# A gated convolution-and-pooling trunk in float32r: the input projection of paired blocks by seven partial products

## The chip, the cores and the metric

The kernel runs on one core of one Trainium2 chip. The metric is device time in microseconds (us) of one execution. Of the core's engines five matter here: TensorE (PE; its weight loads are listed apart as PEld), VectorE (DVE), ScalarE (ACT), GpSimd (POOL) and SyncE (SP). Transfers are issued by SP, ACT or POOL and carried by 16 DMA engines.

## The reference, cut to what matters

There are 1104 tokens: 16 meta tokens and 1024 prompt tokens in one sequence, and 8 samples of 8 tokens. The model width is 1024. One layer is computed:

```
h = RMSNorm(x)                                  # per token, over 1024 channels
z = h @ w_in                                    # 1024 -> 7168, split into seven groups of 1024:
#   a_val | a_gate | a_silu | p_in | p_silu | g_a | g_b
u = a_val * sigmoid(a_gate)                     # GLU
c = causal depthwise conv of u, width 31        # state of 30 positions in front
A = (silu(LayerNorm(c)) * silu(a_silu)) @ w_conv_out
pooled = trailing mean of p_in over 2/4/8/16 positions, minus p_in
B = ((pooled @ w_pool_mix per group) * pool_scale * silu(p_silu)) @ w_pool_out
y = RMSNorm(x + (sigmoid(g_a) * A + sigmoid(g_b) * B) @ w_out)
```

The last 30 values of u and the last 15 of p_in go out as new states. Everything is float32.

## The kernel before

Channels lie on the 128 partitions and tokens along the columns, except in the output projection. Every product is made of three float32r products: a float32 operand is split into a high part (rounded to float32r) and a low part (the remainder), and high x high, high x low and low x high are summed in PSUM. `split` (L97) does that with a ScalarE copy and a VectorE subtraction.

w_in is cut into 56 blocks of 128 output channels, 8 for each of the seven groups. `gemm` (L123) makes one block: 8 chunks of 128 input channels x 3 products x 3 pieces of the tokens, 72 matmuls of 368 columns (all tokens: GLU and pool input) or 364, 362 and 362 columns (without the meta tokens: gates). A block's weights come by one transfer of 512 KB into a tile with two buffers; their two parts have three buffers each. The products of one block fill a PSUM tile of three banks, of which there are two.

In order of the program: the first five pool-input blocks (`NX`) multiply x times the norm's gain, and take the token's factor 1/rms after the product, because the sum over the squares is not ready yet; the statistic is made by small matmuls at `STATS_AT`, and spread over the partitions by others at `SPREAD_AT` (`root_stats` L155, `spread` L169). Then x is normalised and split once for all other blocks (L271 to L276). Then come the pooling branch (`pool_in`, `pool_gates`, `pool_mix`), and blocks in the order that `ORDER` (L42) writes out: GLU with convolution (`glu` L390, `conv_chunk` L367, 30 multiply-adds of 1024 columns and 30 of 64 for each of 8 chunks on VectorE), branch B times its merge gate (`branch_b`), merge gate of A, SiLU path. Results for later wait in DRAM (`d_tb`, `d_sga`). LayerNorm, the merge projection and the output projection with tokens on partitions (`project` L545, matmuls of 512 columns) follow.

The instructions of one engine run in the order in which they were queued. Inside `manual_schedule` that is the program's order; elsewhere a scheduler places what is ready by priority (program order), and `later()` lowers the priority of the convolution by 4000, so that it fills the gaps of VectorE. Tiles of 4.4 KB per partition ("slots", 38) come from one pool.

Of the kernel before, what the change touches and what calls it, by code (L numbers as in the profile page):

```python
# [7 lines left out]
F32 = mybir.dt.float32  # L8
F32R = mybir.dt.float32r
AF = mybir.ActivationFunctionType  # L10
ALU = mybir.AluOpType

P = 128
D = 1024
NK = D // P
META = 16
# [7 lines left out]
TP2 = SEQ  # L24
# [3 lines left out]
# Columns of a PSUM tile's three banks: of all tokens, and of all but the meta tokens. Counts are even.  # L28
CUT1 = (0, N1, 2 * N1, TALL)
CUT2 = (0, 364, 726, T2)  # L30
EW = CB + TP + DB * (CB + DS)
PW = TP + DB * (PB + DS)
# [3 lines left out]
NSLOT = 38  # L36
CONV_LATER = 4000
WARM = 8
NX = 5
STATS_AT, SPREAD_AT = (2, 5), (2, 7)  # L40
# c: GLU and convolution, b: branch B, a: merge gate of A, s: SiLU path of A.
ORDER = "c0 b0 c1 b1 b2 c2 b3 b4 c3 b5 b6 c4 b7 a0 c5 a1 a2 c6 a3 a4 c7 a5 a6 a7 s0 s1 s2"  # L42
# [7 lines left out]
def hybrid_trunk_kernel(  # L50
# [25 lines left out]
    wp = ctx.enter_context(tc.tile_pool(name="wp", bufs=3))  # L76
# [3 lines left out]
    ps3 = ctx.enter_context(tc.tile_pool(name="ps3", bufs=2, space=bass.MemoryType.PSUM))  # L80
    ps1 = ctx.enter_context(tc.tile_pool(name="ps1", bufs=2, space=bass.MemoryType.PSUM))

    def slot(name, n=T2, dt=F32):
        return sl.tile([P, n], dt, tag="slot", name=name, bufs=NSLOT, padded_shape=[P, TALL])

    def bank3(name):
        return ps3.tile([P, 3, 512], F32, tag="bank3", name=name)

    pv = const.tile([P, NPAR], F32, name="pv")
    ident = const.tile([P, P], F32, name="ident")  # L90
    ones = const.tile([P, P], F32, name="ones")
    pool.memset(ones, 1.0 / D)
# [8 lines left out]
    def load_w(src, name):  # L101
        raw = wp.tile([P, NK, P], F32, tag="raw", name=f"raw_{name}", bufs=2)
        h = wp.tile([P, NK, P], F32R, tag="wh", name=f"wh_{name}")
        l = wp.tile([P, NK, P], F32R, tag="wl", name=f"wl_{name}")
        sp.dma_start(out=raw, in_=src)

        def ready():
            split(h, l, raw)
            return h, l

        return ready

    def load_w_now(src, name):
        return load_w(src, name)()
# [7 lines left out]

    def gemm(out, w, xs, c0, cut, ns=range(3), nk=NK, m0=0, ks=None):  # L123
        wh, wl = w
        xh, xl = xs
        for k in ks or range(nk):
            for i, (a, b) in enumerate(((wh, xh), (wh, xl), (wl, xh))):
                for j in ns:
                    pe.matmul(  # L129
                        out[:, j, : cut[j + 1] - cut[j]],  # L130
                        a[:, k, m0 : m0 + P],
                        b[k][:, c0 + cut[j] : c0 + cut[j + 1]],
                        start=(k == 0 and i == 0),
                        stop=(k == nk - 1 and i == 2),
                    )
# [5 lines left out]
    def pieces(ps, t):  # L141
        n, m = CUT2[1], CUT2[2] - CUT2[1]
        return (ps[:, 0, :n], t[:, :n]), (ps[:, 1:, :m], v3(t[:, n:], m))
# [6 lines left out]
    def token_tiles(n):  # L150
        return [min(i * P, n - P) for i in range((n + P - 1) // P)]
# [3 lines left out]
    def root_stats(ssum, n, eps, name):  # L155
        tiles = token_tiles(n)
        nt = len(tiles)
        ps = ps1.tile([P, 512], F32, tag="ps1", name=f"pst_{name}")
        for i, lo in enumerate(tiles):
            pe.matmul(ps[:, 2 * i : 2 * i + 2], ssum[:, lo : lo + P], ones[:, :2], start=True, stop=True)  # L160
        a, r, t = (sm.tile([P, 2 * nt], F32, tag=f"ir{x}", name=f"ir{x}_{name}", bufs=1) for x in "art")
        dve.tensor_scalar(a, ps[:, : 2 * nt], eps, None, ALU.add)
        act.activation(r, a, AF.Sqrt)
        dve.reciprocal(r, r)
        refine(r, a, t)
        return r

    # The factors of root_stats with tokens along the columns, on every partition.
    def spread(r, n, name):  # L169
        tiles = token_tiles(n)  # L170
        nt = len(tiles)
        out = slot(f"ir_{name}", n)
        for g in range(0, nt, 4):
            ps = ps1.tile([P, 512], F32, tag="ps1", name=f"pb_{name}{g}")
            part = tiles[g : g + 4]
            dg = slot(f"dg_{name}{g}", 4 * P)
            for i, lo in enumerate(part):
                d = dg[:, i * P : (i + 1) * P]
                dve.tensor_scalar(d, ident, r[:, 2 * (g + i) : 2 * (g + i) + 1], D, ALU.mult, ALU.mult)
                pe.matmul(ps[:, i * P : (i + 1) * P], ones, d, start=True, stop=True)  # L180
            if len(part) == 4:
                act.copy(out[:, part[0] : part[0] + 512], ps)
            else:
                for i, lo in enumerate(part):
# [481 lines left out]
```

## Time and profile before

| | |
|---|---|
| time, median of 3 runs | 1014.71 us (1014.0 to 1014.74) |
| span of the profiled execution, first to last instruction | 1011.5 us |
| PE busy | 1000.9 us, 5838 matmuls |
| DVE busy | 716.7 us |
| ACT busy | 261.1 us |
| POOL busy | 13.4 us, 29 instructions |
| moved by DMA | 79.02 MB, mean 78 GB/s |

The profiled execution is known by its span; the runs are timed around it, and their median is 3.2 us longer than that span. Busy time is the union of the instructions of an engine; a matmul's own duration (some 330 ns) overlaps the next one's, so the pace of a stream of matmuls is read from the chain, as a stretch's duration over its count.

### The profile page before, as it was taken

Reading aid. Unit: us, or ns where it says so; the run is one execution under the profiler, and the core shown is the slowest. Engines: PE = TensorE matmul, PEld = TensorE weight load, DVE = VectorE, ACT = ScalarE, POOL = GpSimd, SP = SyncE. Lnnn points to the kernel's source line nnn. Section 1 sums busy time; section 2 is a strip of 40 time slices with the busy share of each in tenths; the row PEclk is TensorE's granted clock in tenths of the full one; section 3 lists DMA queues with packets and bytes.
Section 4 is the critical chain, followed back from the end, with each engine's and each line's share of the span. In section 5 each row is a group of like instructions: output and inputs, shape, how many; then the busy total and the mean of one; then the engine's idle time right before and its main releaser. Section 6 shows DMA issues by size and latency. Waiting matters only on the chain.

```text
span 1011.5 us, 13769 instructions
## 1 busy us (share of the span) xinstructions
PE 1000.9 (99%) x5838; PEld 978.2 (97%) x5838; DVE 716.7 (71%) x918; ACT 261.1 (26%) x344; POOL 13.4 (1%) x29
## 2 busy tenths in 40 slices
PE   8999999999999999999999999999999999999997
PEld 7999999999999999999999999999999999997885
DVE  6697753544999959769689799999846934445343
ACT  7644232222211111111121111111245722114111
POOL 0001100000000000000000000000000000000000
PEclk9999999999999999999999999999999999999999
DMA  8222222231212222221221232322111033334322
GB/s 276 68 38 63 61 49 49 45 68 39 48 65 52 90 51 83 69 48 64 70 48 64 68 93 49 101 45 90 64 42 43 23 149 131 130 131 174 124 77 84
DMA packets 45374, 79.02 MB, mean 78 GB/s; under 512 B 22912, under 2 KB 28032, under 8 KB 45312
## 3 DMA queue, kind: packets, MB, share of 16 engines
q1 hardware_dynamic: 43008, 69.22, 23.8%
q10 hardware_dynamic: 2304, 8.91, 2.6%
q8 instruction: 46, 0.75, 0.3%
q14 instruction: 16, 0.13, 0.0%
HBM read 63.09 MB, written 15.03 MB: 77 GB/s over the span
## 4 chain that ended last, share of the span: by engine, by line
PE 96%; DMA 1%; DVE 1%; SPq 0%; issue 0%; ACT 0%; DVEq 0%
PE pg L129 10%; PE pv L129 10%; PE psl L129 9%; PE ppo L129 9%; PE pps L129 9%; PE pga L129 9%; PE pgb L129 9%; PE pco L129 9%; PE pp L129 9%; PE pwo L549 7%; PE pmix L129 2%; DMA raw_wo<-in_w_out 1%; PE pwos L549 1%; DMA raw_p<-in_w_in 1%; DVE wol L99 0%
## 5 line engine op out<-in xcount | busy, mean ns | idle before, releaser
L378 DVE SCALAR_TENSOR_TENSOR c<-ce,pv,c 128x1024 f32<-128x1024 f32 x240 | 307.6, 1283 | 3.1
L379 DVE SCALAR_TENSOR_TENSOR c<-ce,pv,c 128x64 f32<-128x64 f32 x240 | 68.0, 283 | 5.6 <-ACT c L376 1.5
L500 DVE TENSOR_TENSOR lga<-pco,lga 128x364 f32<-128x364 f32 (+1 forms) x16 | 10.8, 719 | 46.8 <-PE pco L129 46.8
L129 PE MATMUL pg<-hh,wh_g 128*128 128x368 f32 x192 | 42.7, 330 | 0.0
L129 PE MATMUL pv<-hh,wh_v 128*128 128x368 f32 x192 | 42.6, 330 | 0.0
L129 PE MATMUL psl<-hh,wl_s 128*128 128x362 f32 (+1 forms) x192 | 42.6, 329 | 0.0
L129 PE MATMUL pg<-hl,wh_g 128*128 128x368 f32 x192 | 42.6, 330 | 0.0
L129 PE MATMUL psl<-hh,wh_s 128*128 128x362 f32 (+1 forms) x192 | 42.6, 329 | 0.0
L129 PE MATMUL pg<-hh,wl_g 128*128 128x368 f32 x192 | 42.6, 330 | 0.0
L129 PE MATMUL pv<-hh,wl_v 128*128 128x368 f32 x192 | 42.5, 330 | 0.0
L129 PE MATMUL pv<-hl,wh_v 128*128 128x368 f32 x192 | 42.5, 329 | 0.0
L129 PE MATMUL ppo<-ql,wh_po 128*128 128x362 f32 (+1 forms) x192 | 42.4, 329 | 0.0
L129 PE MATMUL pps<-hh,wl_ps 128*128 128x362 f32 (+1 forms) x192 | 42.4, 329 | 0.0
L129 PE MATMUL pga<-hh,wl_ga 128*128 128x362 f32 (+1 forms) x192 | 42.4, 329 | 0.0
L129 PE MATMUL pgb<-hh,wl_gb 128*128 128x362 f32 (+1 forms) x192 | 42.3, 328 | 0.0
L129 PE MATMUL ppo<-qh,wl_po 128*128 128x362 f32 (+1 forms) x192 | 42.3, 329 | 0.0
L129 PE MATMUL pco<-cxh,wh_co 128*128 128x362 f32 (+1 forms) x192 | 42.3, 328 | 0.0
L129 PE MATMUL pps<-hl,wh_ps 128*128 128x362 f32 (+1 forms) x192 | 42.2, 328 | 0.0
L129 PE MATMUL pgb<-hl,wh_gb 128*128 128x362 f32 (+1 forms) x192 | 42.2, 328 | 0.0
L129 PE MATMUL pga<-hl,wh_ga 128*128 128x362 f32 (+1 forms) x192 | 42.2, 328 | 0.0
L129 PE MATMUL psl<-hl,wh_s 128*128 128x362 f32 (+1 forms) x192 | 42.2, 328 | 0.0
L129 PE MATMUL pco<-cxl,wh_co 128*128 128x362 f32 (+1 forms) x192 | 42.2, 328 | 0.0
(212 smaller groups left out, 2210.9 us busy)
## 6 DMA issues: line engine op xcount, KB each, us to landing
x<-in_xT SPq DMA_DIRECT2D x24, 184.0 KB, 4.0
d_tb<-gbo ACTq DMA_DIRECT2D x8, 544.0 KB, 2.8
d_sga<-gao ACTq DMA_DIRECT2D x8, 544.0 KB, 3.4
t<-d_tb SPq DMA_DIRECT2D x8, 544.0 KB, 4.5
lga<-d_sga SPq DMA_DIRECT2D x8, 544.0 KB, 5.6
raw_ps<-in_w_in SPq DMA_DIRECT2D x8, 512.0 KB, 3.5
raw_g<-in_w_in SPq DMA_DIRECT2D x8, 512.0 KB, 4.2
raw_v<-in_w_in SPq DMA_DIRECT2D x8, 512.0 KB, 3.5
```

The costliest lines, as they stand in the source:

```text
L129: pe.matmul(out[:, j, : cut[j + 1] - cut[j]], a[:, k, m0 : m0 + P], b[k][:, c0 + cut[j] : c0 + cut[j + 1]], start=(k == 0 and i == 0), sto ...
L378: dve.scalar_tensor_tensor(cp, sp_, wk, cp, ALU.mult, ALU.add)
L379: dve.scalar_tensor_tensor(cs, ss_, wk, cs, ALU.mult, ALU.add)
L500: dve.tensor_tensor(c, p, c, ALU.mult)
L549: pe.matmul(ps[:, n - ns[0], :], x(k), w[k][:, n * 512 : (n + 1) * 512], start=(k == 0 and s == 0), stop=(k == NK - 1 and s == len(passes) ...
```

## The change

Blocks are taken in pairs. Two output blocks, two halves of the input channels (4 chunks each) and two halves of the tokens make a 2 x 2 x 2 product; it is computed by seven products of half size in place of eight (Winograd's form of Strassen's scheme). Columns of tokens are reordered into two halves of 552 (8 meta, 512 prompt and 32 sample tokens each), and a matmul takes half of one half: 276 columns, 272 without the meta tokens.

- Seven token operands ("11", "T3", "21", "T2", "T1", "22", "T4"), with 4 chunks each, are made once after RMSNorm, as sums and differences of the four quarters, and split into two parts: 28 tiles, each of which fills one of now 35 slots.
- Seven weight operands are made for each pair (`w_ops`): two sums by a transfer that adds to its destination, two by VectorE.
- `split_dma` takes the low part by an accumulating transfer from the GpSimd queue: ScalarE writes the high part, then its negative, and the transfer adds the source.
- The products are completed by three PSUM tiles x, y, v of two banks. y starts as ScalarE's copy of x. Two quarters end in PSUM (y after "21", x after "22"), the other two are v combined by VectorE with copies of x taken on the way (c2, c4).
- Six pool-input blocks (four together for the first token half) run plain ahead of the norm's factor; 25 pairs follow, interleaved by hand on PE so that the next pair's first product stands inside the current pair.
- The statistic is now a product with a matrix of ones over full width and its inverse root by logarithm and exponential on ScalarE (`totals`, `inv_root`).
- All of the input projection comes first; pool inputs, gates, SiLU paths and convolution outputs go through DRAM. Mixing, branch B, LayerNorm, merge and output projection follow, on half token ranges (272 columns); their operands are split by `split_dma` as well, except those of the output projection.
- The sample's convolution is a product with a window of 31 and a reduction; the convolution's sum over channels chunks is an accumulating transfer into DRAM.

The core of the diff:

```diff
+    def split_dma(dst_h, dst_l, src):
+        act.copy(dst_h, src)
+        act.mul(dst_l, dst_h.bitcast(F32), -1.0)
+        pool.dma_start(out=dst_l, in_=src, accum_op=ALU.add)
...
-NSLOT = 38
-CONV_LATER = 4000
+NSLOT, NWS, NOP, NZ = 35, 11, 6, 8
+CONV_LATER = 6000
-NX = 5
+NX = 6
+ORDER = "g0 p3 q0 q1 q2 g1 q3 b0 b1 g2 b2 b3 a0 g3 a1 a2 a3 s0 s1 s2 s3"
...
+UNITS1 = ((0, HT // 2), (HT // 2, HT))
+UNITS2 = ((HM, HM + H2 // 2), (HM + H2 // 2, HT))
+UNITS3 = ((0, H2 // 2), (H2 // 2, H2))
...
+    for k in range(NQ):
+        xa, xb = xs[k], xs[NQ + k]
+        dve.scalar_tensor_tensor(xa, xa, col(OFF_NG, k), rms, ALU.mult, ALU.mult)
+        t_split("11", k, xa[:, 0])
+        dve.scalar_tensor_tensor(xb, xb, col(OFF_NG, NQ + k), rms, ALU.mult, ALU.mult)
+        s3, s1, s2, s4 = (half(f"ts{i}{k}") for i in (3, 1, 2, 4))
+        dve.tensor_tensor(s3, xb[:, 1], xa[:, 1], ALU.subtract)
+        t_split("T3", k, s3)
+        dve.tensor_tensor(s1, xa[:, 0], xa[:, 1], ALU.subtract)
+        dve.scalar_tensor_tensor(s2, s1, -1.0, xb[:, 1], ALU.mult, ALU.subtract)
+        t_split("T2", k, s2)
+        t_split("21", k, xb[:, 0])
+        t_split("T1", k, s1)
+        dve.scalar_tensor_tensor(s4, s2, -1.0, xb[:, 0], ALU.mult, ALU.subtract)
+        t_split("22", k, xb[:, 1])
+        t_split("T4", k, s4)
...
+    def w_ops(src, name):
+        a, b, q3, q1, d, q2, q4 = (half_raw(f"{x}_{name}") for x in ("a", "b", "q3", "q1", "d", "q2", "q4"))
+        (a_, b_), (c_, d_) = ((x[:, :NQ], x[:, NQ:]) for x in src)
...
+        sp.dma_start(out=a, in_=a_)
+        sp.dma_start(out=q3, in_=a_)
+        pool.dma_start(out=q3, in_=c_, accum_op=ALU.add)
+        sp.dma_start(out=q1, in_=c_)
+        pool.dma_start(out=q1, in_=d_, accum_op=ALU.add)
+        sp.dma_start(out=b, in_=b_)
+        sp.dma_start(out=d, in_=d_)
+        yield op("a", a)
+        yield op("q3", q3)
+        dve.tensor_tensor(q2, q1, a, ALU.add)
+        yield op("q2", q2)
+        yield op("b", b)
+        yield op("q1", q1)
+        dve.tensor_tensor(q4, q2, b, ALU.add)
+        yield op("q4", q4)
+        yield op("d", d)
...
+        x = bank2(f"px_{name}")
+        product_of(x, "11", True, False)
+        yield
+        y = bank2(f"py_{name}")
+        act.copy(y[:, :, :n], x[:, :, :n])
+        v = bank2(f"pv_{name}")
+        yield
+        product_of(v, "T3", True, False)
+        product_of(x, "T2", False, False)
+        c2 = keep("c2")
+        product_of(y, "21", False, True)
+        put(0, 0, y[:, :, :n])
+        product_of(x, "T1", False, False)
+        c4 = keep("c4")
+        yield
+        dve.scalar_tensor_tensor(c4, v[:, :, :n], -1.0, c4, ALU.mult, ALU.subtract)
+        product_of(x, "22", False, True)
+        put(0, 1, x[:, :, :n])
+        yield
+        put(1, 1, c4)
+        product_of(v, "T4", False, True)
+        dve.scalar_tensor_tensor(c2, v[:, :, :n], -1.0, c2, ALU.mult, ALU.subtract)
+        put(1, 0, c2)
...
+    with tc.manual_schedule(engines={pe.engine}):
+        cur = pairs[0]
+        next(cur), next(cur)
+        for nxt in pairs[1:] + [None]:
+            next(cur)
+            if nxt:
+                next(nxt)
+            next(cur)
+            if nxt:
+                next(nxt)
+            next(cur, None)
+            cur = nxt
...
+        for h in range(2):
+            ps = bank2(f"{name}{h}")
+            gemm(ps, w, lambda k, s: xs[k][h][:, s], UNITS3, tuple(range(nk)), True, True)
+            use(h, ps[:, :, : H2 // 2])
```

In each `product_of`, 4 chunks x 3 products x 2 pieces are 24 matmuls. A letter of `ORDER` is now a pair of blocks: g two sets of seven products (gate and value of the GLU), p, q, b, a, s one. `half_raw` has 11 buffers (`NWS`), the split weight operands 6 (`NOP`).

## Rows read from the trace of the kernel before

**Rows 1.** page, part 1: busy us, share of the span and instructions of each engine
```profile
PE 1000.9 (99%) x5838; PEld 978.2 (97%) x5838; DVE 716.7 (71%) x918; ACT 261.1 (26%) x344; POOL 13.4 (1%) x29
```

**Rows 2.** chain of waits in order of time: start, duration, what (x matmuls)
```profile
40.88 1.90 PE pst_x L160 x18
...
45.93 2.05 PE pb_x L180 x18
...
289.98 12.07 PE pv L129 x72
302.05 11.96 PE pgb L129 x72
...
811.69 95.38 PE pco L129 x576
...
952.08 7.43 PE pwos L549 x32
```

**Rows 3.** busy time by stretch; its column line is shown first
```profile
core 0: us, PE busy (x) PEld busy (x) DVE busy (x) ACT busy (x) POOL busy (x), PEclk, DMA share, GB/s
0.00:5.00 5.00, 3.78 (x16) 3.49 (x16) 0.29 (x1) 2.20 (x4) 0.41 (x5) 1.00 0.49 131
5.00:8.00 3.00, 2.74 (x11) 1.94 (x12) 2.22 (x6) 1.67 (x5) 0.00 (x0) 1.00 0.85 248
8.00:13.00 5.00, 3.40 (x17) 2.29 (x15) 2.77 (x7) 3.38 (x7) 0.00 (x0) 1.00 0.93 311
13.00:25.00 12.00, 12.00 (x71) 11.86 (x72) 11.03 (x21) 11.14 (x21) 0.00 (x0) 1.00 0.95 335
...
230.00:746.00 516.00, 516.00 (x3096) 516.00 (x3095) 434.29 (x573) 87.66 (x106) 4.67 (x12) 1.00 0.23 64
...
1004.00:1011.50 7.50, 0.08 (x1) 0.00 (x0) 2.89 (x9) 0.93 (x3) 0.00 (x0) 0.78 0.19 71
```

**Rows 4.** instruction groups of ScalarE by form: busy, mean ns | idle before
```profile
L98 ACT CAST hh<-x 128x1104 fp32r<-128x1104 f32 x8 | 8.4, 1115 | 0.0
...
L334 ACT ACTIVATE gate<-pps 128x364 f32<-128x364 f32 x8 | 3.7, 467 | 0.0
...
L163 ACT ACT_TABLE_LOAD x2 | 2.6, 1283 | 0.0
L98 ACT CAST mh<-mraw 128x512 fp32r<-128x512 f32 x4 | 2.5, 621 | 4.7 <-DMA mraw<-in_w_mix 4.6
```

**Rows 5.** instruction groups of VectorE by form
```profile
L378 DVE SCALAR_TENSOR_TENSOR c<-ce,pv,c 128x1024 f32<-128x1024 f32 x240 | 307.6, 1283 | 3.1
L379 DVE SCALAR_TENSOR_TENSOR c<-ce,pv,c 128x64 f32<-128x64 f32 x240 | 68.0, 283 | 5.6 <-ACT c L376 1.5
...
L272 DVE SCALAR_TENSOR_TENSOR x<-x,pv,ir_x 128x1104 f32<-128x1104 f32 x8 | 10.3, 1365 | 2.6 <-ACT ir_x L185 2.6
...
L542 DVE TENSOR_SCALAR xr<-xr,s 128x1024 f32<-128x1024 f32 x7 | 5.3, 753 | 0.2
...
L99 DVE TENSOR_TENSOR ml<-mraw,mh 128x512 fp32r<-128x512 f32 x4 | 2.7, 684 | 0.0
```

**Rows 6.** GpSimd in order of time: start, duration, instruction, count
```profile
25.82 0.52 POOL L289 COPY pe<-pst 128x120 f32<-128x120 f32 x2 [24.88 <-DMA pst<-in_spool]
...
109.94 1.49 POOL L289 COPY pe<-pst 128x120 f32<-128x120 f32 x1 [22.92 <-DMA raw_ps<-in_w_in]
...
302.03 0.39 POOL L404 COPY ce<-cst 128x240 f32<-128x240 f32 x1
...
632.63 2.39 POOL L404 COPY ce<-cst 128x240 f32<-128x240 f32 x1
```

**Rows 7.** DMA issues by line: count, KB of each, median us from issue to landing
```profile
mraw<-in_w_mix SPq DMA_DIRECT2D x4, 256.0 KB, 4.3
...
out<-xr SPq DMA_DIRECT2D x2, 256.0 KB, 2.2
```

More of the change, by code (lines that the diff above doesn't have):

```diff
@@ L15 @@
 NK = D // P
+NQ = NK // 2
 META = 16
@@ L148, in refine @@
         dve.scalar_tensor_tensor(r, t, 1.5, r, ALU.add, ALU.mult)
[L150 to L165, printed above, removed]
-        return r
@@ L169, in spread @@
[L169 to L182, printed above, removed]
-            else:
-                for i, lo in enumerate(part):
-                    act.copy(out[:, lo : lo + P], ps[:, i * P : (i + 1) * P])
-        return out
@@ new lines, in hybrid_trunk_kernel, with keep_raw, plain @@
+    for i in range(NF, NX):
+        for lo in (0, NQ):
+            load_first(i, lo, lo + NQ)
+    for k in range(NK):
+        load_x(k, 1, full)
+    def keep_raw(j, h, ps):
+        z = half(f"rawp{j}{h}")
+        act.copy(v3(z, HT // 2), ps[:, :, : HT // 2])
+        sp.dma_start(out=d_raw[j][:, h], in_=z)
+    def plain(out, w, h, ks):
+        gemm(
+            out,
+            lambda k, s: w[s][:, k],
+            lambda k, s: xg[h][k][:, s],
+            UNITS1,
+            ks,
+            ks[0] == 0,
+            ks[-1] == NK - 1,
+        )
@@ new lines, in product, with seven, product_of, keep @@
+    def product(out, w, t, units, first, last):
+        gemm(out, lambda k, s: w[:, s, k], lambda k, s: t[k][:, s], units, tuple(range(NQ)), first, last)
+    def seven(src, name, units, put):
+        ws = w_ops(src, name)
+        n = units[0][1] - units[0][0]
+        def product_of(out, t, first, last):
+            product(out, next(ws), t_ops[t], units, first, last)
+        def keep(what):
+            z = half2(f"{what}_{name}", 2 * n)
+            act.copy(z, x[:, :, :n])
+            return z
+        x = bank2(f"px_{name}")
[21 more added lines that the diff above has]
+        put(1, 0, c2)
@@ L326, in pool_gates @@
[L326 to L339 removed]
+            s2 = slot(f"pw{j}_{d}", (TP,))
@@ new lines, in flat, with pool_pair, put @@
+    def flat(z):
+        return z.rearrange("p a b -> p (a b)")
+    def pool_pair(i):
+        ext = [pool_ext(2 * i + b) for b in range(2)]
+        done = [0, 0]
+        def put(b, h, z):
+            j = 2 * i + b
+            if not b:
+                t = half2(f"zp{j}{h}", HT)
+                act.copy(t, z)
+                z = t
+            r, o = parts(flat(z)), ext[b][2](h)
+            act.copy(o[1], r[1])
+            pool.tensor_copy(o[0], r[0])
+            act.copy(o[2], v3(r[2], DS))
+            done[b] += 1
+            if done[b] == 2:
+                with later():
+                    pool_window(j, *ext[b][:2])
+        return [seven((w_in[PG + 2 * i], w_in[PG + 2 * i + 1]), f"p{i}", UNITS1, put)]
@@ L340, in pool_mix @@
+    q = []
+    for g in range(4):
+        pooled = [halves(fetch(d_pool[j], f"lp{j}"), f"pool{j}") for j in (2 * g, 2 * g + 1)]
+        mraw = slot(f"mraw{g}", (2, 2 * P))
         sp.dma_start(out=mraw, in_=w_mix[g])
-        wm = [wp.tile([P, 2, 2 * P], F32R, tag=f"m{x}", name=f"m{x}{g}", bufs=1) for x in "hl"]
-        split(wm[0], wm[1], mraw)
-        for i, gate in enumerate(gates):
+        wm = op_tile(f"m{g}", (2, 2, 2 * P))
+        split(wm[:, 0], wm[:, 1], mraw)
+        for i in range(2):
```

699 lines of the change are left out of this document (370 added, 329 removed).

## The prediction

> **What bounds the kernel now.** I read the busy shares first: TensorE is at work for 1000.9 of 1011.5 us, VectorE for 716.7, ScalarE for 261.1, GpSimd for 13.4 [rows 1]. A busy share does not say at what pace, so the chain of waits in order of time came next. It runs through matmuls from end to end, and gives paces: a block of 72 matmuls takes 12.07 us with 368 columns (168 ns each) and 11.96 us with 364, 362 and 362 (166.1 ns), 32 matmuls of 512 columns take 7.43 us (232.2 ns) [rows 2]. Busy time by stretch shows where PE is not fed: it starts at 5.0 us, lacks 1.9 us until 13 us, and is done 7.4 us before the end; its granted clock is 1.00, the level of 2.4 GHz, in every stretch but the last [rows 3]. So the end is set by the number of matmuls times their pace, and only these can give time. Summed: 24 blocks x 12.09 + 32 x 11.96 = 672.9 us input projection; branch B and merge projection 191.4; mixing 23.9; output projection 416 x 0.2322 = 96.6; statistics 9.7; together 994.5. With 5.0 of start, 7.4 of tail and 4.6 of gaps that is the span, 1011.5. The median of the runs is 3.2 us longer than the span; I add that at the end.
>
> **The pace of shorter matmuls.** This is the first disputed term, because the change cuts 1104 columns into four pieces in place of three: 6528 matmuls of 272 or 276 columns, and no row has that width. At 2.4 GHz 276 columns need 115.0 ns. The three paces lie 15.0, 14.7 and 18.9 ns above their columns' time [rows 2]. A line through 362.7 and 512 columns gives 5.6 + 0.4426 per column: 127.7 ns at 276, 126.0 at 272. In proportion to the 166.1 ns it would be 126.4 and 124.6; with a fixed 15 ns on top, 130.0 and 128.3. A floor set by loading the weights lies lower: 18 matmuls with 128 x 128 weights and 2 columns took 1.90 us, 105.6 ns each, and 18 of 128 columns (float32) 2.05 us, 113.9 ns [rows 2]. I take the line.
>
> **TensorE's new sum.** Six plain blocks: 6 x 96 = 576 x 127.7 = 73.6 us. A set of seven products has 7 x 24 = 168 matmuls; 9 sets for all tokens (8 GLU, 1 pool) 1512 x 127.7 = 193.1; 16 sets for gates 2688 x 126.0 = 338.7. So the input projection falls from 672.9 to 605.4, though the matmul count for it goes from 4032 to 4776. Branch B and merge 1536 x 126.0 = 193.5, mixing 24.2, output projection 96.6 as before, three column sums 3.0. Total 922.7, 71.8 less than before. By proportional paces 913.7, with the fixed 15 ns 938.
>
> **Start.** Four blocks begin together on 4.5 MB of weights and half of x. The rate reached 335 GB/s at a 0.95 share of the engines [rows 3]; PE's 24.5 us on these blocks need 184. The first chunk comes as before; the second waits for 1.7 MB. I keep 5.0 and 4.6 us, and 1 more.
>
> **The joint where the token operands are made.** PE's own work from 5 us: four blocks of the first half until 33, two more until 45, two blocks of the second half until 57, column sums, then four half blocks until 82.5. The square sums are ready before 57 (ScalarE 8 x 1.12 us after scaling and copies). After the sums' matmuls at 58 come two copies, Ln, Exp and Square of 1104 columns (1.115 us each, by [rows 4], and up to two table loads of 1.283), and four VectorE operations of 0.8 to 1.4 us [rows 5]: the norm's factor is there at about 70. Then each of 4 chunks needs seven operands, each with two ScalarE operations of 552 columns. From 621 ns at 512 columns and 1115 at 1104 [rows 4] one takes 0.654 us, an operand 1.31. The order is by chunk, so the first product ("11", four chunks) waits for the 22nd operand: 71.4 + 22 x 1.31 = 100.2, and for its transfer, 2.2 to 4.3 us for 256 KB [rows 7], so 103. VectorE needs only 5.4 us per chunk and is not the limit. PE runs dry at 82.5: 20 us of stall. Lower bound 5 (the scheduler takes "11" first, and operands follow at PE's pace, 3.1 us per product), upper 45 (weight splits and copies of raw blocks go between, 6 us, and transfers take twice as long). I take 20.
>
> **The sets in steady state.** A set lasts 21.2 to 21.5 us on PE. ScalarE: 14 split operations of 512 columns x 0.621 = 8.7, one copy PSUM to PSUM, two out of PSUM, four activations at 0.62 to 0.65 (467 ns at 364 columns and the slope above [rows 4]) = 4.5; 13.2 us, 62%. VectorE: two weight sums and two combinations, some 2.8 us; the convolution as before 308 us, the sample's taps some 43 in place of 68 [rows 5], windows 54, GLU products 11; together 487 of the 532 us of all sets. The last two chunks (88 us) come in reach with 7 sets (148 us) to go, so LayerNorm is not late. A product takes 3.1 us, and that is the cover of each copy that PE waits for: c2 is taken while "21" runs, c4 and the next y while the next pair's "11" or "T4" runs. Behind a split that waits for its weights these copies queue on ScalarE; before, such waits cost PE nothing from 230 to 746 us [rows 3], with covers four times as long. I take 10 us for all 25 sets, bounds 0 and 50.
>
> **The accumulating transfers, the second disputed term.** No row has one. A gate set moves plainly five weight loads of 262 KB and four results of 278 KB, 2.42 MB, and adds nine times 262 KB, 2.36 MB. At 335/0.95 = 353 GB/s [rows 3] that is 6.9 us plus 6.7 us times f, f being the price of an added byte against a copied one. An add has one stream more to read: f of 1 to 2 is what I expect, and up to 20.3 us of 21.2. I cost it at nothing on the path, with f open up to 3 for the range.
> GpSimd issues nine of these per set, 324 in all, where it had 29 instructions. Its copies of 120 columns took 0.26 us when VectorE was between jobs and 1.49 in the pooling windows; one of 240 took 0.39 or 2.39 beside the convolution [rows 6]. Nine times 0.26 to 2.39 is 2.3 to 21.5 us, within a set. Behind a waiting issue stand the other operands' issues, but six split operands are five products ahead.
> The Trainium skill (SBUF — State Buffer, "Who interferes with whom") says that a VectorE instruction with two SBUF inputs holds up a GpSimd instruction that reads SBUF, while descriptor writing is held up only by VectorE's two-port modes. The stretched copies agree with its first half; that the issues stay short beside the convolution no row here shows. By that rule issuing would be near the 2.3 us, and the sum is unchanged.
>
> **Mixing, merge, end.** Splits of pooled inputs and of q take 16 x 4 x 0.65 = 42 us of ScalarE around 24 us of PE; a third can be done ahead, since the 28 operand tiles leave seven slots until the last products free more. I take 8 us of stall (0 to 20). Branch B's 97 us cover LayerNorm and A's splits (65 us of ScalarE). Output weights come late for the same lack of slots: 2 us (0 to 10). Tail 7.4.
>
> **Sum.** 922.7 + 5.0 + 5.6 + 20 + 10 + 8 + 2 + 7.4 = 980.7 of span, and 3.2: 984. Its own range, from the bounds of the stalls and paces taken singly, is 950 to 1010.
>
> **Rivals.**
> *Everything hides* (0.14): proportional pace 913.7, a stall of 5 at the operands, 3 elsewhere: 942. For it speaks that PE lost nothing at any joint before [rows 3]; against it ScalarE's 28.8 us at the operands.
> *The transfers become the bound* (0.11): PE waits in each set. It is slower than before once f passes 2.3: gate sets then take 22.3 us (16 x 1.1 = 18) and the operands, 22 x 283 KB, 41 in place of 29 us (+12), which is the whole gain of 31. At f = 3 it is 16 x 5.8 + 9 x 2.4 + 24 = 138 more, 1122. For it: nine of eighteen transfers of a set are of a kind without a row; against it: the share was 0.23 in the steady part [rows 3].
> *Issuing on GpSimd binds* (0.06): at 2.39 us each [rows 6] the sets just keep pace, but the operands' 22 issues take 53 us and not 29: with 5 at the sets, 1013, no change.
> *The pace does not fall* (0.04): each nanosecond per short matmul is 6.5 us, so at 132.4 ns for 276 columns the gain is gone; at 145 it is 1097. The row at 105.6 ns speaks against it.
> *The joints add up* (0.07): operands 45, sets 40, mixing 20 us: 1051.
>
> **How the numbers follow.** The forecast holds 0.58. Faster by over 0.2%, which is about what a measurement tells from no change: 0.58 + 0.14 and a third of the GpSimd case, 0.74; within 0.2%: 0.03; slower 0.23. The range of 8 in 10 reaches from 945 to 1060: it leaves out the transfers' case beyond f = 2.6, half of the unchanged pace and a third of the lowest case, 0.18.
>
> **What would show it.** Pace: 168 matmuls of a gate set in 21.2 us, in the chain. Operands: an idle stretch of PE near 20 us before the first "11", ended by ScalarE or a transfer. Sets: PE idle per set under 0.5 us, DMA share under 0.9. Wrong: PE idle in every set and ended by a transfer (f too high) or by ScalarE (its queue), or 132 ns and more per matmul.

## The result: slower, 1671 us, and the profile after

The changed kernel takes 1671.28 us (median of four executions, 1657.32 to 1677.56); the kernel before, beside it, 1014.63. The ratio is 1.6451 [1.638, 1.6522]. The profiled execution took 1672.76 us, with a span of 1671.0.

Busy time of each engine from the page of the kernel after, the line that answers to [rows 1]:

```profile
PE 1019.5 (61%) x6960; PEld 980.7 (59%) x6960; DVE 663.3 (40%) x807; ACT 560.5 (34%) x934; POOL 299.1 (18%) x370
```

TensorE's busy time is 19 us more than before, and 97 us more than the forecast sum of 922.7, in a span that is 660 us longer. So most of the loss is not in the matmuls: TensorE was kept waiting. How the waits lie shows in busy time by stretch, with the columns of [rows 3]:

```profile
core 0: us, PE busy (x) PEld busy (x) DVE busy (x) ACT busy (x) POOL busy (x), PEclk, DMA share, GB/s
400.00:450.00 50.00, 43.51 (x338) 42.62 (x336) 5.50 (x8) 23.54 (x39) 16.69 (x19) 1.00 0.87 183
500.00:550.00 50.00, 0.00 (x0) 0.00 (x0) 50.00 (x47) 0.00 (x0) 0.88 (x1) 0.50 0.11 22
600.00:650.00 50.00, 45.52 (x352) 44.63 (x352) 5.51 (x8) 24.02 (x41) 15.84 (x19) 1.00 0.85 178
1112.00:1192.00 80.00, 35.07 (x197) 32.27 (x196) 15.25 (x20) 38.24 (x63) 24.27 (x28) 0.68 0.92 233
1192.00:1380.00 188.00, 108.94 (x777) 106.60 (x777) 55.84 (x52) 63.90 (x76) 21.76 (x25) 0.76 0.57 158
1380.00:1564.00 184.00, 120.34 (x771) 116.54 (x769) 35.48 (x49) 25.08 (x31) 6.14 (x8) 0.79 0.39 113
```

Read the first three lines together. In 400 to 450 and 600 to 650 us the sets come nearest to the forecast: PE is busy for 44 and 46 of 50 us at the full granted clock, which is some 2 to 3 us short in each set, and VectorE for 5.5. In 500 to 550 PE does nothing, ScalarE does nothing, and VectorE is busy for all 50. The work is there, but it is not spread. The granted clock fell to 0.50, the level of 1.2 GHz, in the stretch in which PE stood still, and was 0.90 in the next. Behind the sets, mixing, branch B and the merge projection take 80, 188 and 184 us for 24, 97 and 97 us of matmuls; the output projection takes 99 us, near its pace.

What TensorE waited for (engine, tile and line, what it waited for: us in total, times, longest):

```profile
PE px_a L143 <- ACT c_a L374: 84.2, 1, 84.2
PE px_q L143 <- ACT c_q L374: 75.8, 2, 72.4
PE ppo L143 <- ACT wh_po L111: 74.1, 6, 32.0
PE px_p L143 <- ACT c_p L374: 73.9, 2, 70.6
PE px_b L143 <- ACT c_b L374: 72.8, 2, 68.2
PE px_g L143 <- ACT c_g L374: 54.3, 1, 54.3
```

Four single waits of 68 to 84 us and one of 54 stand in the sets, all put down to ScalarE's copy of x (line 374). That copy takes 0.6 us, so the question is what stands ahead of it. Three timelines at one of the four (start, duration, instruction, count, idle before and releaser): TensorE, VectorE, ScalarE:

```profile
477.98 3.20 PE L143 MATMUL px_b<-t,woa_b 128*128 128x272 f32 x24
553.59 4.55 PE L143 MATMUL px_q<-t,woq_q 128*128 128x272 f32 x24 [72.41 <-ACT c_q L374]
```

```profile
482.95 59.88 DVE L504 SCALAR_TENSOR_TENSOR c<-ce,pv,c 128x1024 f32<-128x1024 f32 x50
...
553.57 0.72 DVE L392 SCALAR_TENSOR_TENSOR c_q<-pv_q,c_q 128x544 f32<-128x544 f32 x1 [0.91 <-ACT c_q L374]
```

```profile
552.69 0.35 ACT L514 ACTIVATE c<-c,pv 128x64 f32<-128x64 f32 x1 [77.47 <-DVE c L513]
552.95 0.59 ACT L374 COPY c_q<-px_q 128x544 f32<-128x544 f32 x1
```

VectorE takes 50 taps of the convolution in a row, then four more between the sample's products, until 552.7 us; the combination that frees a PSUM tile (line 392) comes after the last. ScalarE has the sample's bias (line 514, 0.35 us) in its queue, which needs the end of the same chunk, and the copy for TensorE behind it. The first product behind the wait took 4.55 us where the one before it took 3.20, with the granted clock at 0.50 in the stretch before it: a wait costs somewhat more than its length, and a part of the 97 us of busy time above is this. GpSimd stands the same way in front of a chunk's sum (tile d_csum), with the next sets' transfers behind:

```profile
POOL d_csum L521 <- DVE c L504: 184.8, 3, 66.1
```

### The profile page after: what moved, and what is told of

It is laid out like the page before. It is cut to its first block, busy times and chain, and to the rows that moved or that the text cites. A ratio compares the mean times of both kernels' runs of the same rounds, so it can differ in the third digit from the quotient of the medians.

```text
span 1671.0 us, 18045 instructions
## 1 busy us (share of the span) xinstructions
PE 1019.5 (61%) x6960; PEld 980.7 (59%) x6960; DVE 663.3 (40%) x807; ACT 560.5 (34%) x934; POOL 299.1 (18%) x370
## 4 chain that ended last, share of the span: by engine, by line
issue 19%; PE 18%; DMA 12%; POOL 2%; ACT 2%; DVE 1%; POOLq 0%; SPq 0%; DVEq 0%; ACTq 0%
PE ppo L143 6%; PE pwo L741 6%; DMA woq_a<-q_a 2%; PE px_s L143 1%; DMA wl_po<-raw_po 1%; DMA pool<-lp 1%; DMA woq_s<-q_s 1%; DMA q_s<-in_w_in 1%; PE pv_s L143 1%; PE pco L143 1%; PE px_a L143 1%; PE pmix L143 1%; DMA raw_po<-in_w_po 1%; DMA q_a<-in_w_in 1%; DMA wob_a<-b_a 1%
## 5 line engine op out<-in xcount | busy, mean ns | idle before, releaser
L143 PE MATMUL ppo<-q,wh_po 128*128 128x272 f32 x512 | 93.1, 309 | 74.1 <-ACT wh_po L111 74.1
L143 PEld LDWEIGHTS ppo<-q,wh_po 128*128 128x128 f32 x512 | 79.5, 207 | 75.7 <-ACT wh_po L111 75.7
L143 PE MATMUL pco<-cx,wh_co 128*128 128x272 f32 x512 | 98.6, 324 | 22.4 <-ACT wh_co L111 22.4
L143 PEld LDWEIGHTS pco<-cx,wh_co 128*128 128x128 f32 x512 | 85.9, 224 | 24.0 <-ACT wh_co L111 24.0
L143 PE MATMUL pco<-cx,wl_co 128*128 128x272 f32 x256 | 60.5, 327 | 38.3 <-DMA wl_co<-raw_co 38.3
L143 PEld LDWEIGHTS pco<-cx,wl_co 128*128 128x128 f32 x256 | 47.1, 223 | 40.4 <-DMA wl_co<-raw_co 40.4
L143 PE MATMUL pp<-xg,wh_p 128*128 128x276 f32 x384 | 65.9, 293 | 0.9 <-ACT total_x L168 0.5
L143 PE MATMUL pmix<-pool,m 128*128 128x272 f32 x192 | 34.5, 345 | 41.8 <-ACT m L106 23.6
L143 PE MATMUL ppo<-q,wl_po 128*128 128x272 f32 x256 | 54.5, 300 | 8.1 <-DMA wl_po<-raw_po 8.1
L143 PEld LDWEIGHTS pmix<-pool,m 128*128 128x128 f32 x192 | 31.7, 238 | 44.3 <-ACT m L106 24.2
```

Source lines behind the costliest of these rows:

```text
L143: pe.matmul(out[:, u, : hi - lo], w(k, a), xs(k, b)[:, lo:hi], start=first and k == ks[0] and i == 0, stop=last and k == ks[-1] and i == 2 ...
```

## The experiments

The changed kernel's own executions lie up to 20 us apart and each experiment is one execution, so differences below that are not read. "The sets" are the stretch from the end of the plain blocks (82 us) to the last set.

**1. The taps handed out.** Theory: the order in VectorE's queue. The taps of a chunk are traced one by one, behind instructions that they must follow on VectorE.

```diff
+DOSE = (4, 5)
...
+    def behind(ins, n):
+        with later(), tc.issue_after(ins.ins):
+            drain(n)
...
-        dve.scalar_tensor_tensor(c4, v[:, :, :n], -1.0, c4, ALU.mult, ALU.subtract)
+        ins = dve.scalar_tensor_tensor(c4, v[:, :, :n], -1.0, c4, ALU.mult, ALU.subtract)
+        behind(ins, DOSE[0])
...
-                with later():
-                    conv_chunk(j, e, es)
+                waiting.append(conv_chunk(j, e, es))
```

> Same instructions as the changed kernel, but the convolution's taps, which stand about 54 in a row in VectorE's queue four times, are handed out: 4 behind each first combination of a set (line 392), 5 behind each second one (line 398). Theory (order in VectorE's queue): each run of 54 taps is about 54 x 1.28 = 69 us in which the combinations that TensorE needs cannot be issued, and ScalarE and GpSimd wait in order behind the chunk's last sums; TensorE's waits for ScalarE at the head of four sets (about 70 us each, 295 us in all) fall under 80 us together, and the time to 1350 to 1420 us. Rival (the accumulating transfers are too slow for the sets, by their landing time or by GpSimd's issuing): the same transfers are made, so the time stays within 1600 to 1680 us and the waits move to weight operands.

Measured: 1414.31 us, 257 less. The four waits are gone (px_a's is left with 13 us); what tops the list now lies in the operand stage and behind the sets:

```profile
PE ppo L144 <- ACT wh_po L112: 80.1, 6, 32.0
PE px_g L144 <- ACT c_g L387: 51.4, 1, 51.4
...
PE px_a L144 <- ACT c_a L387: 13.2, 3, 9.1
```

The sets still took 751 us, 30 for each, although single products run at the forecast pace. Something else holds them.

**2. Taps left out.** The other way to the same question:

```diff
-                dve.scalar_tensor_tensor(cp, sp_, wk[:, k : k + 1], cp, ALU.mult, ALU.add)
+                if k < 3:
+                    dve.scalar_tensor_tensor(cp, sp_, wk[:, k : k + 1], cp, ALU.mult, ALU.add)
```

> 28 of the 30 VectorE taps of each of the eight convolution chunks are left out, so the convolution and what follows from it have other values; all else is as in the changed kernel. Theory (order in VectorE's queue): the four waits of about 70 us go, and with them 280 to 340 us; time 1320 to 1400 us. Rival (transfers or GpSimd): below 60 us goes, time above 1610 us.

Measured: 1393.09 us, 278 less. With 28 of 30 taps gone it gains 21 us more than with all of them handed out, and none of that in the sets. These take 751 us either way, though VectorE is busy for 407 us in the one and 196 in the other (columns as above, the handed-out taps first):

```profile
82.00:832.00 750.00, 576.25 (x4203) 567.33 (x4204) 407.19 (x471) 356.52 (x615) 234.05 (x288) 0.88 0.83 179
```

```profile
82.00:833.00 751.00, 572.14 (x4204) 563.52 (x4204) 196.01 (x320) 356.97 (x620) 233.04 (x291) 0.88 0.85 183
```

The 21 us lie in mixing (81 us against 99), where the handed-out taps go on until 917 us. So in the sets it was the order of the taps that cost, not their work; and what still holds the sets is not VectorE's load.

**3. Which queue blocks.** Handing out moves VectorE's combinations and ScalarE's bias together. Here ScalarE's instruction goes and the run stays:

```diff
-        act.activation(cs, cs, AF.Identity, bias=col(OFF_CB, i))
+        dve.tensor_scalar(cs, cs, col(OFF_CB, i), None, ALU.add)
```

> As the changed kernel (1671 us, taps in runs), but the sample's bias (line 514), a ScalarE instruction of 64 columns that waits for the end of a run of taps (232 us in four times) with the copies for TensorE behind it, is an addition on VectorE. Theory (VectorE's own run holds the combinations of lines 392 and 398, whichever engine is behind it): TensorE gets one copy earlier but then waits for the combination that frees its PSUM tile; time falls by less than 80 us, the four waits turn from ScalarE's copy to VectorE's combination. Rival (the one ScalarE instruction is the block, VectorE's combinations are not late): the time falls by 200 us or more, to 1470 us or less.

Measured: 1655.86 us, no difference that can be told. Three of the four waits only change their name, from ScalarE's copy to VectorE's combination:

```profile
PE px_a L143 <- ACT c_a L374: 81.5, 1, 81.5
PE pv_b L143 <- DVE c_b L392: 77.4, 4, 67.2
...
PE pv_q L143 <- DVE c_q L392: 72.3, 3, 66.3
PE pv_p L143 <- DVE c_p L392: 67.1, 1, 67.1
```

The fourth, px_a, stays under ScalarE's name, but not for the bias: its copy stands behind a split for the mixing stage, which waits for the taps itself:

```profile
930.06 0.65 ACT L111 CAST pool<-lp 128x544 fp32r<-128x544 f32 x1 [54.68 <-DVE c L504]
```

So VectorE's run is enough to hold TensorE. A list of waits names the last releaser; here two queues were blocked by the same run, and it named one that could be cleared without any gain. Whether GpSimd's wait for the same taps would have held the sets by itself was not tried.

**4. The sets' weight operands without transfers.**

```diff
-            split_dma(o[:, 0], o[:, 1], x)
+            split(o[:, 0], o[:, 1], x)
```

> The low parts of the sets' weight operands are made by ScalarE and VectorE (copy, subtract) instead of by a negated copy and an accumulating transfer; 7 transfers of 256 KB per set go, 7 subtractions of 1024 elements on VectorE per set come. The taps stay in runs of about 55. Theory (order in VectorE's queue): the four long waits stay, time within 5% of the changed kernel, 1590 to 1750 us. Rival (accumulating transfers bound the sets): the sets run at TensorE's pace and the time falls by 250 us or more, to 1420 us or less.

(An operand is 512 columns in the trace, 0.69 us on VectorE; the expectation has it twice as large.) Measured: 1548.72 us, 123 less, all of it in the sets, and between the two. The four waits stay, at 58 to 71 us, so the order is no matter of transfers, though together they are 48 us shorter; the small waits between them (VectorE's combinations 34 us, transfers of weights 11) are gone. There are two causes, and I had named one.

**5. Behind the sets, without transfers.**

```diff
-        split_dma(h, l, raw)
+        split(h, l, raw)
...
-    def halves(t, name, how=split_dma):
+    def halves(t, name, how=split):
```

> Behind the sets (mixing and the two output projections) every low part is made by ScalarE and VectorE instead of by an accumulating transfer; the sets are as in the changed kernel. Theory (in these stages the chain copy, negated copy, GpSimd's issue, transfer of about 5 us is longer than a block's matmuls, and GpSimd waits in order): the two projections, 188 and 184 us in the changed kernel, fall to 110 to 140 us each, the time to 1530 to 1600 us. Rival (ScalarE's order alone does it: each block's weight copies stand behind the split that waits for the block before): the projections stay above 165 us each and the time within 40 us of 1671.

Measured: 1558.42 us, 113 less. Mixing takes 50 us in place of 79, branch B 169, merge 134: half-way. (17 of the 113 us lie in the sets, which the edit leaves as they were; that is within the spread between executions.) ScalarE's timeline inside merge shows what is left:

```profile
1391.93 0.65 ACT L106 CAST mx<-lga 128x544 fp32r<-128x544 f32 x1 [9.77 <-DVE lga L695]
1397.89 0.64 ACT L106 CAST mx<-lga 128x544 fp32r<-128x544 f32 x1 [5.32 <-DVE lga L695]
1398.44 1.04 ACT L106 CAST wh_co<-raw_co 128x1024 fp32r<-128x1024 f32 x1
```

The copy of a block's weights (wh_co) stands behind the two splits of the block before (mx), which wait for that block's last product. In each block the weights come too late by their own split.

**6. Weights ahead.** On top of 1: raw weights in tiles of their own and not in slots, splits without transfers, two blocks ahead; mixing one group ahead.

```diff
+    def next_w():
+        while to_load and len(ahead) < 3:
+            ahead.append(load_w(*to_load.pop(0)))
+        return ahead.pop(0)
```

> As the kernel with the taps handed out (1414 us), and behind the sets: low parts by ScalarE and VectorE, the weight blocks of the two projections loaded into tiles of their own and split two blocks ahead of their use, the mixing's operands one group ahead. Theory (order: in the two projections each block's weight copies stand in ScalarE's queue behind splits and LayerNorm steps that wait for the block before; splitting alone left 168 and 134 us of 97): the projections take 100 to 115 us each, mixing under 60, time 1170 to 1230 us. Rival (the splits' work itself is too much for ScalarE and VectorE in these stages): projections stay above 130 us each, time 1270 us or more.

Measured: 1278.61 us, 136 less than 1414. Mixing takes 54 us and merge 97, its pace. Branch B takes 174, as under the rival, but not for its reason: LayerNorm's steps still stand between its blocks on VectorE (29.8 us of waits), and TensorE waits for the sum that LayerNorm's mean needs, because the last handed-out tap of the convolution runs only at 947 us, 105 behind the sets:

```profile
PE pt_m L168 <- ACT sumh_m L107: 37.4, 1, 37.4
```

**7. Token operands without transfers, pool windows handed out.** On top of 1; the doses now go by time, 5.2 and 8.0 us, and are larger.

```diff
-        split_dma(t[:, 0], t[:, 1], src)
+        split(t[:, 0], t[:, 1], src)
...
-    for j in range(NX):
-        with later():
-            pool_raw(j)
+    waiting += [pool_raw(j) for j in range(NX)]
```

> As the kernel with the taps handed out (1414 us), and two parts of the operand stage changed: the low parts of the 28 token operands by ScalarE and VectorE (subtract) instead of 28 accumulating transfers of 276 KB; the pool windows of the six raw blocks handed out behind the sets' combinations by time (5.2 us behind the first, 8.0 us behind the second), as the taps. Theory (the stage from 82 to 210 us, in which TensorE stands 86 us, is 28 transfers on engines that are then full, and then VectorE's queue with the raw blocks' windows ahead of the combinations): waits for t<-x (35 us) and for c_g (51 us) fall under 30 us together; time 1330 to 1370 us. Rival (the stage is bound by the operand sums on VectorE themselves, 28 subtractions more make it longer): the stage stays at 80 us or more, time 1400 us or more.

Measured: 1410.02 us against 1414.31, no difference that can be told. The named waits fell (t by transfer 30 to 0, c_g 51 to 8), and others took their place: px_v 34.6, pv_q 28.4. The rival's number came, but not by its reason.

**8. The edits of 1, 6 and 7 together, then with that of 4 as well.**

> Both of the two before: taps and windows handed out, token operands by subtraction, projections' weights ahead. Only the sets' weight operands and sums still come by accumulating transfers. Theory: the parts add; time 1090 to 1160 us, the sets without waits over 15 us. Rival (what is cleared in one stage is given back in another, the transfers or VectorE bounding the sets): 1200 us or more.

> As the run with all of it, and the sets' weight operands too by ScalarE and VectorE; the two weight sums per set stay with accumulating transfers. Against the run with all: theory (transfers cost little once the queues' order is right; VectorE, busy 456 of 750 us in the sets, gets 175 subtractions of 1.2 us more = 210 us and becomes the bound of the sets): 0 to 60 us slower. Rival (transfers of 256 KB, landing 4 to 7 us behind the copy, cost the sets 4 us each): 60 to 110 us faster.

Measured: 1230.05 and 1111.57 us. The first is 184 us under 1414, more than the 136 and 4 of the two edits taken singly. Against 6 it is 49 less, of which 38 lie in branch B (174 us to 137) and 4 in the sets: with the larger doses the last tap runs at 836 us, inside the sets, and the wait for the mean is gone. With the order mended the sets still took 755 us; taking the weight operands' transfers out brought them to 636 and the time down by 118, more than the rival's 60 to 110. Both rivals were right in kind: the first run stayed above 1200 because the transfers held the sets.

**9. A plain copy in place of the accumulation.** What of the 118 us is the accumulation itself? As the first run of 8; the negated copy stays, and the transfer writes over it:

```diff
-            split_dma(o[:, 0], o[:, 1], x)
+            act.copy(o[:, 0], x)
+            act.mul(o[:, 1], o[:, 0].bitcast(F32), -1.0)
+            pool.dma_start(out=o[:, 1], in_=x.bitcast(F32R))
```

> As the run with taps and windows handed out, token operands by subtraction and projections' weights ahead (1230 us), but the transfers that make the low parts of the sets' weight operands are plain copies of the same 256 KB from the same queue, without accumulation (the low parts then hold the raw weights, so every set's product has other values). Tells what of the 118 us that went with these transfers is the accumulation's longer hold on the DMA engines and what is the way there: GpSimd's issuing in order, the negated copy, the landing. Theory (hold: per MB the accumulating queue holds the engines 1.8 times as long as the other, and the DMA share of the sets is 0.80): share falls to about 0.65 and the time by 50 us or more, to 1180 us or less. Rival (the way there: issue in order behind waits): time within 25 us of 1230.

Measured: 1161.31 us, 69 less. The queues in the sets (packets, MB, share of 16 engines; q0 is GpSimd's), in the order accumulating, plain, none:

```profile
q0 software_dynamic: 31596, 59.28, 46.0%
q1 hardware_dynamic: 74448, 71.60, 33.2%
```

```profile
q1 hardware_dynamic: 74448, 71.60, 37.1%
q0 software_dynamic: 31536, 59.19, 33.8%
```

```profile
q1 hardware_dynamic: 74304, 71.32, 40.9%
q0 software_dynamic: 7200, 14.88, 15.1%
```

Without the weight operands GpSimd's queue holds the engines for 0.151 x 636 = 96 us (weight sums and the convolution's sum). If these are the same 96 in the other two, the 44.4 MB of the operands held them for 0.460 x 755 - 96 = 251 us when accumulating and 0.338 x 688 - 96 = 137 us when copied: a factor of 1.84, as an estimate. The 69 us are not the engines' hold alone, though, for a plain copy is also issued faster by GpSimd, by some 0.3 us (first the accumulating run):

```profile
L114 POOL DMA_DIRECT2D woq_s<-q_s x16 | 14.5, 904 | 34.6 <-ACT woq_s L113 24.0 <-issue 4.7 <-ACT wob_s L112 4.5
```

```profile
L342 POOL DMA_DIRECT2D woq_s<-q_s x16 | 9.1, 570 | 32.1 <-ACT woq_s L341 30.5 <-PE px_s L144 0.9 <-issue 0.7
```

In the sets GpSimd is busy for 210 us in the one and 153 in the other; no run separates the two. The other 50 of the 118 us are what a plain copy still costs: its own hold of 137 us, ScalarE's negated copy, GpSimd's issue, the landing. These are not separated either.

**10. LayerNorm handed out, a mixture, GpSimd, later windows.** Four attempts at the rest, from the second run of 8: LayerNorm's chunks behind the blocks of branch B; on top of this, three operands of seven by transfers again; or two of seven subtracted on GpSimd; or the raw blocks' windows behind the convolutions, with larger doses (6.0 and 9.0 us), alone and with GpSimd.

```diff
+            ins = dve.tensor_tensor(of_half(o, h), ps, of_half(o, h), ALU.mult)
+            if h and then:
+                with tc.issue_after(ins.ins):
+                    for i in then:
+                        step(i)
...
+            (split if what in ('a', 'q3', 'q2', 'q4') else split_dma)(o[:, 0], o[:, 1], x)
...
+            if what in ("b", "d"):
+                act.copy(o[:, 0], x)
+                pool.tensor_tensor(o[:, 1], x, o[:, 0].bitcast(F32), ALU.subtract)
...
+                waiting.append(conv_chunk(j, e, es))
+                if j < NX:
+                    waiting.append(pool_raw(j))
```

> As the run with the sets' weight operands by subtraction too (1112 us), and LayerNorm's steps handed out in the pool projection: the mean ahead of its first block, two chunks behind each of the first four blocks' products on VectorE, the scaling of the chunks behind the last three. Theory (the projection, 137 us of 97, waits 32 us for VectorE's product of a block that stands behind a run of LayerNorm steps): projection 100 to 110 us, time 1075 to 1090 us. Rival (LayerNorm's work itself is what is late, and TensorE then waits for the normalised chunks ahead of the last projection): time above 1100 us.

> As the run with LayerNorm handed out, but three of the seven weight operands of each set (b, q1, d) by accumulating transfers again: VectorE loses 75 subtractions (some 90 us of 578 in the sets of 636 us), the DMA engines get 75 transfers of 256 KB. Theory (both resources bound the sets, VectorE at 0.91 and the DMA engines at 0.80 in the two extremes; in between each has room): 10 to 40 us faster than the run with LayerNorm handed out. Rival (any accumulating transfer is on the path, by ScalarE's and GpSimd's order): 20 us or more slower.

> As the run with LayerNorm handed out (1105 us), but the low parts of two of the seven weight operands of each set (b, d) by a subtraction on GpSimd, which is busy 65 of 632 us there, instead of on VectorE, which is busy 577. Theory (VectorE's queue, nearly full, holds back the combinations): 50 subtractions of 1.2 us less on VectorE, 15 to 40 us faster. Rival (GpSimd's subtraction is several times as long as VectorE's and slows VectorE's own instructions beside it, or TensorE's pace alone bounds the sets from 310 us on): within 15 us, or slower.

> As the run with LayerNorm handed out (1105 us), but the pool windows of the six raw blocks no longer stand first in the list that is handed out behind the combinations: each stands behind a convolution chunk (6.0 and 9.0 us a time instead of 5.2 and 8.0). There the sets take TensorE's pace from 310 us on, but between 82 and 310 us TensorE has 144 us of matmuls in 228. Theory (the windows' loads of raw blocks and of the inverse root come late, and VectorE waits for them in order, so that the combinations stand behind): the 84 us fall to 40 to 55, time 1060 to 1080 us. Rival (the operands themselves, 28 splits and 20 sums on ScalarE and VectorE, hold the stage): within 12 us of 1105.

> Both of the two others of this call: windows of the raw blocks behind the convolutions, two low parts per set on GpSimd. Theory: their gains add, 1035 to 1065 us, so the operand joint and VectorE's load are what is left over the kernel before. Rival: no better than the better of the two, 1060 us or more.

Measured: 1104.92, 1169.71, 1128.19, 1148.93 and 1166.10 us. The first shortened branch B from 137 to 114 us and lost most of it beside it (12 us ahead of its first block, where TensorE now waits 11 for the mean's sum, and merge 104 in place of 97): 7 us, not to be told from none. All four others are slower, GpSimd's subtractions by 23 us only. The mixture's rival holds: with three transfers the sets lose 69 us (702 in place of 632) at a DMA share of only 0.65, so it is not the engines' occupation alone. On GpSimd a subtraction takes 1.55 to 2.0 us (means of four) in place of VectorE's 0.69, and VectorE, rid of 50 (34 us), gets 22 us longer taps. VectorE's taps and GpSimd's operand (busy, mean ns | idle) in that run, then the taps without it:

```profile
L531 DVE SCALAR_TENSOR_TENSOR c<-ce,pv,c 128x1024 f32<-128x1024 f32 x240 | 329.1, 1374 | 2.6
```

```profile
L342 POOL TENSOR_TENSOR wob_q<-b_q,wob_q 128x512 fp32r<-128x512 f32 x4 | 8.0, 2003 | 19.9 <-ACT wob_q L341 19.8
```

```profile
L527 DVE SCALAR_TENSOR_TENSOR c<-ce,pv,c 128x1024 f32<-128x1024 f32 x240 | 307.0, 1281 | 1.6
```

The Trainium skill (SBUF — State Buffer, "Who interferes with whom") says that a VectorE instruction with two SBUF inputs and a GpSimd instruction that reads SBUF contend, and that of two that contend the one issued first keeps the port and the other waits. The taps, 1.281 us alone and 1.374 beside the subtractions, agree. Its other half, which the page calls inferred and the prediction left open, is that descriptor writing is not held up by such instructions. It agrees too: GpSimd's issues of the tiles woq took 0.88 to 0.93 us each in the changed kernel and 0.90 to 0.92 with the taps handed out beside them.

The last question was the stretch from 82 to 310 us, here of the run with LayerNorm handed out (with the stretch from 310 us to the end of the sets beside it) and of the one with later windows:

```profile
110.00:160.00 50.00, 34.07 (x251) 33.63 (x249) 26.04 (x44) 13.41 (x22) 5.10 (x8) 0.86 0.69 156
160.00:210.00 50.00, 35.45 (x228) 35.02 (x229) 33.15 (x54) 15.12 (x30) 9.54 (x17) 0.80 0.80 163
82.00:310.00 228.00, 164.58 (x1142) 160.75 (x1142) 184.03 (x256) 78.20 (x137) 22.45 (x34) 0.84 0.54 122
310.00:714.00 404.00, 390.47 (x3062) 387.45 (x3061) 392.49 (x480) 163.41 (x286) 42.63 (x56) 1.00 0.57 146
```

```profile
110.00:160.00 50.00, 50.00 (x395) 50.00 (x394) 26.73 (x37) 22.40 (x40) 6.16 (x8) 1.00 0.38 85
160.00:210.00 50.00, 22.27 (x160) 21.83 (x158) 47.67 (x58) 8.82 (x17) 3.56 (x6) 0.74 0.34 81
82.00:310.00 228.00, 168.46 (x1250) 166.27 (x1249) 185.10 (x246) 84.37 (x146) 19.18 (x31) 0.85 0.44 108
```

With later windows PE is full from 110 to 160, and then stands for one wait of 32 us (px_q, from ScalarE's copy) from 160 to 210. At 310 us this run is ahead, with 1250 matmuls done against 1142, some 14 us; from there to the end of the sets it loses 59, in waits of 1 to 13 us for copies and combinations. The loss moved; it did not go. Since the doses are larger too, the windows' place alone is not shown to cost this. What orders this stretch well is left open.

## Why the prediction was wrong, by its steps

**The pace** held. In the timeline of TensorE one product of 276 columns begins 3.05 us behind the other:

```profile
413.26 3.21 PE L143 MATMUL px_g<-tT,woq_g 128*128 128x276 f32 x24
416.31 3.21 PE L143 MATMUL py_g<-t,wob_g 128*128 128x276 f32 x24
```

That is 127.1 ns for each of 24 matmuls, and 125.4 with 272 columns; the line through [rows 2] gave 127.7 and 126.0. TensorE's new sum, 922.7 us, was sound, and not what decides.

**The sets in steady state: "I take 10 us for all 25 sets, bounds 0 and 50". This step failed.** The sets took 1030 us from 82 us on. VectorE's load had been added up (487 of 532 us) and found to fit, with the convolution to fill the gaps. But a queue is not a sum: a run of 54 taps is 69 us, as long as three sets, and a set needs VectorE twice, with c2 and c4. The forecast gave a product's 3.1 us as the cover of the copies that PE waits for, and never asked what may stand ahead of the combinations. This was worth 257 us (experiment 1), VectorE's run being enough to hold TensorE (3). Why the scheduler put the taps into one gap was not tried.

**The accumulating transfers: "I cost it at nothing on the path".** The price f, forecast at 1 to 2, is 1.84. The sum around it was short: forecast 6.9 + 6.7 x 1.84 = 19.2 us per set. Measured, in the first run of 8: a DMA share of 0.80 times 755 us, over 25 sets, is 24.2 us, more than TensorE's 21.3, in sets of 30.2. By this sum a set could not keep TensorE's pace even with full engines, and they were not full. Plain bytes took 3.5 us per MB (0.332 x 755 / 71.6) in place of 2.83, and there were 2.9 MB per set in place of 2.42, with the loads and stores of pool, convolution and samples that the term left out. So the rival "the transfers become the bound" was right in kind, at f = 1.84 and not at 2.3: taking the weight operands' transfers away gave 118 to 123 us, with or without the order mended. Of this 69 go with the accumulation, by the engines' hold and the longer issue together. The rival on GpSimd's issuing did not come as it was put: an issue took 0.9 to 1.2 us, not 2.39, and GpSimd was busy for 210 of 755 us.

**The joint: 20 us, bounds 5 and 45.** The operands themselves held PE for 28.2 us by transfers and 6.3 by ScalarE, inside the bounds. Behind them came a wait of 54 us, which no term had, for ScalarE's copy c_g. That copy waited for VectorE's work on the raw blocks' windows:

```profile
187.39 0.62 ACT L374 COPY c_g<-px_g 128x552 f32<-128x552 f32 x1 [52.28 <-DVE pes L455]
```

Line 455 multiplies a raw block by the norm's factor, out of tiles that by the program share their eight buffers (`NZ`) with the copy's target; so it was most likely a buffer that came free late, and not the order of a queue. With windows handed out and operands by subtraction (7) the wait is 8 us; the buffers alone were not tried. Even in the best version 84 us are lost between 82 and 310 us, where PE has 144 us of matmuls.

**Mixing, merge, end.** "Branch B's 97 us cover LayerNorm" and 8 us at mixing: mixing and the two projections took 452 us for 218 us of matmuls. The cover was a sum again. Weight copies stood on ScalarE behind LayerNorm's squares and behind splits that wait for the block before, and raw weights waited for slots. Order and transfers together were worth 136 us here (6).

Put in a row: 1671, taps 257 less, stages behind the sets 136 less, the edits of 7 another 49 less (first run of 8 against 6; 38 of it in branch B, where the last taps no longer run late, and hardly any in the operand stage that the edits were meant for), weight operands 118 less, LayerNorm 7 less: 1105, 91 us over the kernel before and 121 over the forecast. By stage that is some 71 in the sets, 30 around mixing, 17 in branch B, 7 in merge. From 310 us to the end of the sets, this version runs 3062 matmuls in 404 us, 131.9 ns each, near the forecast pace, and there VectorE is busy for some 97% of the time: the transfers' work, taken back on VectorE, leaves little room for what is still out of order. No version here beats the kernel before.

## What to carry to other kernels

An engine's busy time summed over a stage says whether work fits, not when it is done: for each instruction that the bounding engine waits for, ask how long the longest run is that may stand ahead of it in its own queue, and hand filler work out in doses that its cover can bear. A transfer that takes work off an engine has to be priced with all traffic of the stage, at the rate seen under load. When a list of waits names a short instruction, look at what stands ahead of it, and take that away alone before believing it.

## What the runs showed of the hardware

- An accumulating transfer of 256 KB within SBUF, issued by GpSimd, held the DMA engines some 1.84 times as long as a plain copy of the same bytes from the same queue (5.66 against 3.08 us per MB of 16 engines, estimated as in 9). GpSimd issued it in 0.90 to 1.00 us, the plain copy in 0.57 to 0.63 (means of the tiles woq, sixteen issues each). In the changed kernel's sets the accumulating ones landed 4.7 to 6.1 us after their issue (medians of the same tiles).
- GpSimd's subtraction of 128 x 512 took 1.55 to 2.0 us against VectorE's 0.69, and VectorE's taps took 1.374 us beside it in place of 1.281.
